# Eight matmuls with the high parts, then eight with the low parts, in place of eight pairs

## The chip, the cores and the metric

The kernel runs on one core of one Trainium2 chip. The metric is the device time of one execution in microseconds; lower is better. Three executions of the kernel before took 1486.58, 1487.91 and 1487.88 us, median 1487.88.

## The reference

One decoder block on 256 tokens of width 2048, in float32. What matters here is which matrix products it holds, and in which order:

```python
h = rmsnorm(x, attn_norm[i])
z = h @ w_in[i]                      # split into mq, mk, mv, mo, mi, mf, aq, ak, av, gm, ga
...                                  # mLSTM branch -> hm, attention branch -> ha
merged = (jax.nn.sigmoid(gm) * (hm @ w_up_m[i])
          + jax.nn.sigmoid(ga) * (ha @ w_up_a[i]))
x = x + merged @ w_out[i]
h = rmsnorm(x, mlp_norm[i])
x = x + jnp.square(jax.nn.relu(h @ w_ff1[i])) @ w_ff2[i]
h = rmsnorm(x, ple_norm[i])
x = x + jax.nn.sigmoid(h @ w_ple_gate[i]) * (p[i] @ w_ple_proj[i])
return rmsnorm(x, final_norm)
```

`w_ff1` is 2048 x 8192 and `w_ff2` 8192 x 2048; these two hold most of the arithmetic.

## The kernel before

**Split numbers.** A float32 value is held as two `float32r` values, high and low, whose sum is close to it. The product of a weight and an activation is taken as high x high + high x low + low x high. An activation tile `blk` is 128 x 512: columns 0 to 255 (`[:, 0:T]`, T = 256 tokens) hold the high part, columns 256 to 511 the low part. So one matmul with the weight's high part `h` as the stationary operand and the whole `blk` as the moving one (512 columns) gives high x high and high x low, side by side in one PSUM bank, and one with the weight's low part `l` and the left half of `blk` (256 columns) adds low x high to the left half.

**Chunks.** All weights are read in an order set by `plan()`, in chunks of 128 x 1024 (512 KB), two to a DMA. For chunk i+3 (`LOOK` = 3), `prep` lets ACT cast the chunk to `wh` (L182) and `prep_rest` lets DVE subtract to get `wl` (L190). There are four buffers each of `wh` and `wl`. The loop in `run()` goes through the chunks; for each it emits the PE's matmuls, then side work (`side()`), then the evacuation of banks that are complete.

**Two kinds of group.** In the groups named in `ROWS` (av, mv, mo, gm, um, ga, ua) the activations are stationary and the weights move, always 512 columns; the change doesn't touch them. In all other groups, called tile groups here (mq, mk, gate, aq, ak, wo, f1, f2, pp, pg), a chunk holds eight 128 x 128 weight tiles, called units: eight steps of the contraction into one PSUM bank (four outputs with two steps each for pp). Per unit the PE gets the high matmul and then the low one. Two groups differ: gate has no low matmul, and the last group, pg 3 (`narrow`), takes the high x high and high x low products as two matmuls of 256 columns, so that a unit is three matmuls of 256 columns. Every matmul has its own weight load (LDWEIGHTS, PEld in the profile).

**What sets the order.** Each engine runs its instructions in the order in which the loop emits them. Beside the loop, generators (attention, mLSTM, merge, statistics) put their work between chunks by a planner that keeps its own clock per engine; they put some matmuls and transposes on the PE, always between chunks. `wo` 0, the first group after the merge, takes its first four chunks in the order 0, 2, 1, 3 (`turn`), since its chunks 1 and 3 need the blocks that the merge makes last. `f2` needs the blocks `hid` that f1 makes, f1 the blocks `u2` that `next_operand` makes after wo.

Of the kernel before, what the change touches and what calls it, by code (L numbers as in the profile page):

```python
# [24 lines left out]
T = 256  # L25
# [26 lines left out]
def plan():  # L52

    g = []
    for n in range(2):
        g.append(("av", n))
    g += [("mq", 0), ("mk", 0), ("gate", 0), ("mv", 0), ("mv", 1), ("mo", 0), ("mo", 1)]
    for n in range(2):
        g += [("aq", n), ("ak", n)]
    for n in range(4):  # L60
        g += [("gm", n), ("um", n)]
    for n in range(4):
        g += [("ga", n), ("ua", n)]
    for n in range(4):
        g.append(("wo", n))
    for j in range(4):
        g += [("f1", 4 * j + n) for n in range(4)] + [("f2", 4 * j + n) for n in range(4)]
    for n in range(4):
        g += [("pp", n), ("pg", n)]
    return g  # L70


def turn(name, n, c):


    return (0, 2, 1, 3)[c] if (name, n) == ("wo", 0) and c < 4 else c
# [43 lines left out]
class Block:  # L120
# [788 lines left out]
    def run(self):  # L909
        nc, d = self.nc, self.d  # L910
        groups = plan()
        chunks = []
        for name, n in groups:
            c = {"gate": 2, "um": 4, "ua": 4, "pp": 1}.get(name, 8)
            chunks += [(name, n, i, c) for i in range(c)]
        self.nchunk = len(chunks)
        self.names = [c[0] for c in chunks]
        assert self.nchunk == 2 * d["w"].shape[0]
        self.stage, self.w, self.val, self.acc, self.rb, self.rcol = {}, {}, {}, {}, {}, {}
        self.summed = {}  # L920
        self.opd = {k: {} for k in ("u1", "u2", "u3", "hm", "ha", "mg", "p")}
        for j in range(4):
            self.opd["hid", j] = {}

        self.ones = self.cp.tile([128, 128], F32, name="ones")
        nc.vector.memset(self.ones, 1.0)
        self.warm_up()
        nc.scalar.preload_act_table_set("sqrt_and_others")
        self.x = {q: self.new4() for q in range(4)}
        self.dma(0, False)  # L930
        self.load_x(0, 0, 1)
        self.cols = self.cp.tile([128, NCOL], F32, name="cols")
        nc.scalar.dma_start(out=self.cols, in_=d["cols"])
        self.load_w(0, 0, 512)
        self.load_x(0, 1, 2)
        self.load_w(0, 512, 1024)
        self.load_x(0, 2, 3)
        self.load_w(0, 1024, 1536)
        self.load_x(0, 3, 4)
        self.load_w(0, 1536, 2048)  # L940
        for i in range(2, 8):
            if i < 2 * STAGE and i % 2 == 0:
                self.dma(i // 2, False)
            self.load_x(i // 2, 2 * (i % 2), 2 * (i % 2) + 2)
            if i < 2 * STAGE:
                self.load_w(i // 2, 1024 * (i % 2), 1024 * (i % 2) + 1024)
        self.con = self.cp.tile([128, NCON], F32, name="con")
        self.ident = self.con[:, K_ID:K_ID + 128]
        self.maskA = self.con[:, K_CA:K_CA + 256]
        self.maskB = self.con[:, K_CB:K_CB + 384]  # L950
        self.ones4 = self.cp.tile([4, T], F32, name="ones4")
        nc.vector.memset(self.ones4, 1.0)

        def load_u(k):
            self.opd["u1"][k] = self.blk()
            self.split(self.opd["u1"][k], self.xt(k), self.col(C_G1 + k))

        for i in range(LOOK):
            self.prep(i, 2)
            l, s, h = self.rest  # L960
            self.rest = None
            for k in range(2):
                load_u(2 * i + k)
                c = slice(512 * k, 512 * k + 512)
                self.copy(h[:, c], s[:, c])
                self.tt(l[:, c], s[:, c], h[:, c].bitcast(F32), OP.subtract)
            if i == 1:
                self.dma(STAGE)
        self.spawn(self.first_stats())
        self.spawn(self.tables())  # L970
        banks, acc = {}, {}
        for i, (name, n, c, nch) in enumerate(chunks):
            self.now = i
            if 2 * i + 7 < 16:
                load_u(2 * i + 6)
                load_u(2 * i + 7)
            if c == 0 and name == "ua":
                self.x[n] = self.new4()
                self.load_x(n, 0, 4)
            if i == 2:  # L980
                nc.sync.dma_start(out=self.con, in_=d["con"])
            if c == 0 and (name, n) == ("f2", 8):
                self.spawn(self.load_p())
            self.prep(i + LOOK)
            h, l = self.w.pop(i)
            src = self.opd[self.operand(name, n)]
            units, out = self.units(name, turn(name, n, c)), []
            for m, k in units:
                while k not in src:
                    self.force((name, n, c))  # L990
            if name in ROWS:
                nk = self.depth(name)
                if c == 0:
                    banks = [self.new_bank() for _ in range(2)]
                order = [(u, p, b) for u in range(2) for p in range(3) for b in range(2)]
                if c == nch - 1:
                    order = [(u, p, b) for b in range(2) for u in range(2) for p in range(3)]
                for u, p, b in order:
                    k = units[u][1]
                    wt = (h, h, l)[p][:, 512 * u:512 * u + 512]  # L1000
                    o = T * (p == 1) + 128 * b
                    self.mm(banks[b], src[k][:, o:o + 128], wt, start=k == 0 and p == 0,
                            stop=k == nk - 1 and p == 2)
                if c == nch - 1:
                    f = {"av": self.evac_v, "mv": self.evac_v, "mo": self.evac_o}
                    out.append((f.get(name, self.evac_t), name, n, banks))
            else:
                nk = self.depth(name)
                for u, (m, k) in enumerate(units):
                    if k == 0:  # L1010
                        acc[m] = self.new_bank()
                    ps = acc[m]
                    wc = slice(128 * u, 128 * u + 128)
                    a = src[k]
                    if self.narrow(name, n):
                        self.mm(ps[:, 0:T], h[:, wc], a[:, 0:T], start=k == 0, stop=False)
                        self.mm(ps[:, 0:T], h[:, wc], a[:, T:], start=False, stop=False)
                    else:
                        self.mm(ps, h[:, wc], a, start=k == 0,
                                stop=name == "gate" and k == nk - 1)  # L1020
                    if name != "gate":
                        self.mm(ps[:, 0:T], l[:, wc], a[:, 0:T], start=False, stop=k == nk - 1)
                    if k == nk - 1:
                        out.append((self.evac, name, n, m, ps))
            self.side()
            self.prep_rest(i + LOOK)
            for f, *args in out:
                f(*args)
        while self.tasks:
            self.force("end")  # L1030
        self.finish()
# [65 lines left out]
```

## Time and profile before

| | |
|---|---|
| three executions | 1486.58, 1487.91, 1487.88 us |
| the profiled execution | 1489.35 us, its span 1487.3 us |
| PE (matmuls) busy | 1472.3 us, 99% of the span |
| PEld (weight loads) busy | 1274.1 us, 86% |
| DVE, ACT busy | 992.0 us (67%), 736.4 us (50%) |
| granted TensorE clock | 0.996 of full speed in the mean |
| HBM | 187 GB/s over the span |

A matmul is recorded from its start to a modelled end, and the next one starts before that end. So the time that a matmul takes from the PE is read here as the distance between the starts of neighbours, not from its recorded duration.

### The profile page before, as it was taken

The page shows a single profiled execution, that of the slowest core. Times are in us where ns is not written, and L with a number is a line of the kernel's source. Part 1 is how long each engine was busy: PE and PEld are TensorE (multiplying, and loading weights), DVE is VectorE, ACT ScalarE, POOL GpSimd, SP SyncE. Part 2 cuts the span into 40 slices and gives each one's busy share as a digit, 9 for nine tenths or more (in the row PEclk, how much of TensorE's full clock was granted, in tenths as well). Part 3 has the DMA queues.
Part 4 walks back from the last instruction along what each step waited for, and adds up shares of the span by engine and source line. Part 5 has one row for each costly group of instructions (what it writes and reads, how often), then busy time and mean ns, then how long its engine had stood idle before and what let it go on. Part 6 is the DMA issues. An engine that isn't in the chain of part 4 may idle for free.

```text
span 1487.3 us, 19861 instructions
## 1 busy us (share of the span) xinstructions
PE 1472.3 (99%) x7996; PEld 1274.1 (86%) x7996; DVE 992.0 (67%) x1479; ACT 736.4 (50%) x1026; POOL 0.2 (0%) x4
## 2 busy tenths in 40 slices
PE   9999999999999999999999999999999999999996
PEld 7888888888888888888888888888888888888886
DVE  7686558875445556777766677656766667777785
ACT  7565654554444444455443454334444345555663
POOL 0000000000000000000000000000000000000000
PEclk9999999999999999999999999999999999999998
DMA  8554454444555554545455555555554555555551
GB/s 316 190 198 169 162 194 170 171 170 171 198 198 205 193 221 173 198 170 198 181 191 194 188 184 195 199 184 184 198 198 180 195 190 182 194 199 184 184 198 57
DMA packets 41467, 279.89 MB, mean 188 GB/s; under 512 B 4736, under 2 KB 5536, under 8 KB 8608
## 3 DMA queue, kind: packets, MB, share of 16 engines
q1 hardware_dynamic: 41232, 278.58, 52.3%
q8 instruction: 62, 1.02, 0.3%
q14 instruction: 29, 0.24, 0.1%
q10 hardware_dynamic: 144, 0.06, 0.0%
HBM read 276.52 MB, written 2.10 MB: 187 GB/s over the span
## 4 chain that ended last, share of the span: by engine, by line
PE 98%; DVE 1%; DMA 0%; ACT 0%; SPq 0%; issue 0%; DVEq 0%
PE acc L222 98%; PE acc L226 1%; DMA wst<-w 0%; DVE g L190 0%; ACT wh L182 0%; ACT blk L182 0%; DVE blk L190 0%; ACT L867 0%; SPq L360 0%; DVE rd L190 0%; DVE z L190 0%; ACT sq L178 0%; SPq L329 0%; ACT z L178 0%; DVEq L1092 0%
## 5 line engine op out<-in xcount | busy, mean ns | idle before, releaser
L222 PE MATMUL acc<-blk,wh 128*128 128x512 f32 (+1 forms) x3056 | 1041.7, 388 | 0.7 <-DVE blk L190 0.7
L222 PE MATMUL acc<-blk,wl 128*128 128x256 f32 x2976 | 832.4, 280 | 0.0
L190 DVE TENSOR_TENSOR wl<-wst,wh 128x1024 fp32r<-128x1024 f32 (+1 forms) x519 | 630.8, 1217 | 302.3 <-ACT wh L182 292.0
L182 ACT CAST wh<-wst 128x1024 fp32r<-128x1024 f32 (+1 forms) x521 | 544.6, 1046 | 461.5 <-PE acc L222 402.0
L222 PEld LDWEIGHTS acc<-blk,wh 128*128 128x128 f32 x3056 | 568.0, 187 | 124.3 <-DVE blk L190 1.4
L222 PEld LDWEIGHTS acc<-blk,wl 128*128 128x128 f32 x2976 | 562.0, 189 | 0.2
L222 PE MATMUL acc<-wh,blk 128*128 128x512 f32 x1152 | 318.7, 392 | 0.5 <-ACT wh L182 0.4
L222 PEld LDWEIGHTS acc<-wh,blk 128*128 128x128 f32 x1152 | 215.3, 188 | 45.5 <-ACT wh L182 1.6
L222 PE MATMUL acc<-wl,blk 128*128 128x512 f32 x576 | 184.8, 390 | 0.0
L222 PEld LDWEIGHTS acc<-wl,blk 128*128 128x128 f32 x576 | 108.0, 188 | 23.2 <-DVE wl L190 0.4
L182 ACT COPY lo<-acc 128x256 f32<-128x256 f32 (+1 forms) x118 | 43.0, 372 | 153.5 <-PE acc L222 153.5
L190 DVE TENSOR_TENSOR g<-g,acc 128x256 f32<-128x256 f32 (+2 forms) x166 | 72.1, 437 | 48.6 <-PE acc L222 45.9
L190 DVE TENSOR_TENSOR z<-acc,lo 128x256 f32<-128x256 f32 x76 | 32.3, 424 | 67.1 <-ACT lo L182 67.1
L182 ACT CAST blk<-z 128x256 fp32r<-128x256 f32 x64 | 26.0, 406 | 29.0 <-DVE z L201 29.0
L190 DVE TENSOR_TENSOR z<-z,rb 128x256 f32<-128x256 f32 x76 | 32.3, 425 | 3.2 <-ACT rb L182 0.6
L201 DVE SCALAR_TENSOR_TENSOR z<-z 128x256 f32<-128x256 f32 x64 | 27.3, 426 | 2.2
L178 ACT ACTIVATE sq<-g 128x256 f32<-128x256 f32 x64 | 25.9, 409 | 5.2 <-DVE g L190 4.5
L190 DVE TENSOR_TENSOR blk<-z,blk 128x256 fp32r<-128x256 f32 x64 | 26.7, 417 | 0.0
L190 DVE TENSOR_TENSOR nacc<-nacc,sq 128x256 f32<-128x256 f32 x59 | 24.8, 421 | 2.4 <-ACT sq L178 1.5
L178 ACT ACTIVATE blk<-g,cols 128x256 fp32r<-128x256 f32 x48 | 23.9, 508 | 3.0 <-DMA cols<-cols 1.5
L201 DVE SCALAR_TENSOR_TENSOR blk<-g,cols,blk 128x256 fp32r<-128x256 f32 x48 | 22.6, 479 | 3.6 <-ACT blk L178 3.6
L182 ACT CAST blk<-acc 128x256 fp32r<-128x256 f32 x24 | 9.0, 373 | 26.5 <-PE acc L226 13.1
(118 smaller groups left out, 333.6 us busy)
## 6 DMA issues: line engine op xcount, KB each, us to landing
wst<-w SPq DMA_DIRECT2D x256, 1024.0 KB, 4.8
wst<-w SPq DMA_DIRECT2D x4, 512.0 KB, 6.8
g<-x SPq DMA_DIRECT2D x4, 512.0 KB, 5.7
g<-x SPq DMA_DIRECT2D x6, 256.0 KB, 6.8
out_dram<-g SPq DMA_DIRECT2D x3, 512.0 KB, 2.8
wst<-w SPq DMA_DIRECT2D x4, 256.0 KB, 5.5
g<-x SPq DMA_DIRECT2D x4, 128.0 KB, 5.1
con<-con SPq DMA_DIRECT2D x1, 385.0 KB, 8.1
```

What stands on the lines that cost most here:

```text
L178: self.nc.scalar.activation(out, in_, func, **kw)
L182: self.nc.scalar.copy(out, in_)
L190: self.nc.vector.tensor_tensor(out, a, b, op=op)
L201: self.nc.vector.scalar_tensor_tensor(out, a, s, b, op0, op1)
L222: self.nc.tensor.matmul(out, lhsT=lhsT, rhs=rhs, start=start, stop=stop)
L226: self.nc.tensor.transpose(out, in_, ident)
```

## The change

In each chunk of a tile group the loop over the units now runs twice: first it emits all high matmuls (the 512-column ones, or the two of 256 columns in pg 3), then all low ones. The instructions, their number, operands and sizes stay as they are. Evacuation is still noted when the last step of a bank has its low matmul.

```diff
-                for u, (m, k) in enumerate(units):
-                    if k == 0:
-                        acc[m] = self.new_bank()
-                    ps = acc[m]
-                    wc = slice(128 * u, 128 * u + 128)
-                    a = src[k]
-                    if self.narrow(name, n):
-                        self.mm(ps[:, 0:T], h[:, wc], a[:, 0:T], start=k == 0, stop=False)
-                        self.mm(ps[:, 0:T], h[:, wc], a[:, T:], start=False, stop=False)
-                    else:
-                        self.mm(ps, h[:, wc], a, start=k == 0,
-                                stop=name == "gate" and k == nk - 1)
-                    if name != "gate":
-                        self.mm(ps[:, 0:T], l[:, wc], a[:, 0:T], start=False, stop=k == nk - 1)
-                    if k == nk - 1:
-                        out.append((self.evac, name, n, m, ps))
+                for low in (False, True):
+                    for u, (m, k) in enumerate(units):
+                        if k == 0 and not low:
+                            acc[m] = self.new_bank()
+                        ps = acc[m]
+                        wc = slice(128 * u, 128 * u + 128)
+                        a = src[k]
+                        if low:
+                            if name != "gate":
+                                self.mm(ps[:, 0:T], l[:, wc], a[:, 0:T], start=False,
+                                        stop=k == nk - 1)
+                            if k == nk - 1:
+                                out.append((self.evac, name, n, m, ps))
+                        elif self.narrow(name, n):
+                            self.mm(ps[:, 0:T], h[:, wc], a[:, 0:T], start=k == 0, stop=False)
+                            self.mm(ps[:, 0:T], h[:, wc], a[:, T:], start=False, stop=False)
+                        else:
+                            self.mm(ps, h[:, wc], a, start=k == 0,
+                                    stop=name == "gate" and k == nk - 1)
```

On the PE, the third chunk of `wo` 0 stood like this before, behind the merge's eight transposes (L226). `acc_4596` is the PSUM bank, `wh_4575` and `wl_4576` are the chunk's high and low weights, the `blk` tiles the merged blocks 8 to 15; block 12 is `blk_4644` and block 15, the last to be made, `blk_4661`:

```order
L226 MATMUL acc_4653<-con_119,g4_4516 128x128 x4
L222 MATMUL acc_4596<-blk_4397,wh_4575 128x512
L222 MATMUL acc_4596<-blk_4397,wl_4576 128x256
L222 MATMUL acc_4596<-blk_4400,wh_4575 128x512
L222 MATMUL acc_4596<-blk_4400,wl_4576 128x256
...
L222 MATMUL acc_4596<-blk_4658,wh_4575 128x512
L222 MATMUL acc_4596<-blk_4658,wl_4576 128x256
L222 MATMUL acc_4596<-blk_4661,wh_4575 128x512
L222 MATMUL acc_4596<-blk_4661,wl_4576 128x256
L222 MATMUL acc_4621<-blk_4397,wh_4593 128x512
```

And now, in the same place:

```order
L226 MATMUL acc_4653<-con_119,g4_4516 128x128 x4
L222 MATMUL acc_4596<-blk_4397,wh_4575 128x512
L222 MATMUL acc_4596<-blk_4400,wh_4575 128x512
...
L222 MATMUL acc_4596<-blk_4658,wh_4575 128x512
L222 MATMUL acc_4596<-blk_4661,wh_4575 128x512
L222 MATMUL acc_4596<-blk_4397,wl_4576 128x256
L222 MATMUL acc_4596<-blk_4400,wl_4576 128x256
...
L222 MATMUL acc_4596<-blk_4661,wl_4576 128x256
L222 MATMUL acc_4621<-blk_4397,wh_4593 128x512
```

The matmul that needs block 15 moved from the fifteenth place of the chunk to the eighth, and behind it stand eight low matmuls where one stood.

In the last chunk of pg 3, the end of the PE's work on weights, these rows stood before (a row with x2 is the high x high and the high x low product of one unit):

```order
L222 MATMUL acc_12781<-blk_11730,wh_12719 128x256 x2
L222 MATMUL acc_12781<-blk_11730,wl_12720 128x256
L222 MATMUL acc_12781<-blk_11784,wh_12719 128x256 x2
L222 MATMUL acc_12781<-blk_11784,wl_12720 128x256
L222 MATMUL acc_12846<-ones_78,nacc_11916 128x1
```

And now:

```order
L222 MATMUL acc_12781<-blk_11784,wh_12719 128x256 x2
L222 MATMUL acc_12781<-blk_11424,wl_12720 128x256
...
L222 MATMUL acc_12781<-blk_11730,wl_12720 128x256
L222 MATMUL acc_12781<-blk_11784,wl_12720 128x256
L222 MATMUL acc_12846<-ones_78,nacc_11916 128x1
```

All matmuls of this chunk have 256 columns in both; only their order moved, and the last one is the same.

## Rows read from the trace of the kernel before

**Rows 1.** The page: busy time by engine; the chain that ended last.

```profile
PE 1472.3 (99%) x7996; PEld 1274.1 (86%) x7996; DVE 992.0 (67%) x1479; ACT 736.4 (50%) x1026; POOL 0.2 (0%) x4
PE 98%; DVE 1%; DMA 0%; ACT 0%; SPq 0%; issue 0%; DVEq 0%
```

**Rows 2.** Waits of the PE and one of ACT: total us, times, longest.

```profile
PE acc L222 <- DVE blk L190: 0.7, 2, 0.5
...
ACT wh L182 <- PE acc L222: 402.0, 301, 2.7
```

**Rows 3.** Matmuls and weight loads by shape: count, busy us, mean recorded ns.

```profile
L222 PE MATMUL acc<-blk,wh 128*128 128x512 f32 x2928 | 1018.7, 393 | 0.7 <-DVE blk L190 0.7
L222 PE MATMUL acc<-blk,wl 128*128 128x256 f32 x2976 | 832.4, 280 | 0.0
...
L222 PEld LDWEIGHTS acc<-blk,wl 128*128 128x128 f32 x2976 | 562.0, 189 | 0.2
```

**Rows 4.** Timeline, PE, in f1: pairs (start, recorded us).

```profile
699.82 0.39 PE L222 MATMUL acc<-blk,wh 128*128 128x512 f32 x1
700.05 0.28 PE L222 MATMUL acc<-blk,wl 128*128 128x256 f32 x1
...
705.72 0.39 PE L222 MATMUL acc<-blk,wh 128*128 128x512 f32 x1
```

**Rows 5.** One stretch of f1 and f2: PE busy, matmuls, granted clock, DMA share.

```profile
700.00:900.00 200.00, 200.00 (x1155) 1.00 0.53 190
```

**Rows 6.** Timeline, PE, gate: sixteen 512-column matmuls behind pairs, from two windows.

```profile
96.50 3.82 PE L222 MATMUL acc<-blk,wh 128*128 128x512 f32 x16
...
98.11 2.20 PE L222 MATMUL acc<-blk,wh 128*128 128x512 f32 x9
100.15 0.39 PE L222 MATMUL acc<-wh,blk 128*128 128x512 f32 x1
```

**Rows 7.** Timeline, PE, start of pg 3: 256-column matmuls behind pairs.

```profile
1448.86 0.40 PE L222 MATMUL acc<-blk,wh 128*128 128x256 f32 x2
...
1449.80 0.28 PE L222 MATMUL acc<-blk,wl 128*128 128x256 f32 x1
1450.16 0.28 PE L222 MATMUL acc<-blk,wl 128*128 128x256 f32 x1
...
1451.96 0.28 PE L222 MATMUL acc<-blk,wl 128*128 128x256 f32 x1
```

**Rows 8.** Timeline, PE: first pair of wo, and the end of its sixteenth.

```profile
566.77 0.39 PE L222 MATMUL acc<-blk,wh 128*128 128x512 f32 x1
...
572.42 1.04 PE L226 MATMUL acc<-con,g 128*128 128x128 f32 x8
```

**Rows 9.** Timeline, PE, in aq/ak: eleven pairs.

```profile
198.13 0.39 PE L222 MATMUL acc<-blk,wh 128*128 128x512 f32 x1
...
202.00 0.40 PE L222 MATMUL acc<-blk,wh 128*128 128x512 f32 x1
```

**Rows 10.** Timeline, PE, third chunk of wo 0 [idle before, releaser].

```profile
573.21 0.47 PE L222 MATMUL acc<-blk,wh 128*128 128x512 f32 x1
...
576.88 0.50 PE L222 MATMUL acc<-blk,wh 128*128 128x512 f32 x1 [0.24 <-DVE blk L190]
577.22 0.28 PE L222 MATMUL acc<-blk,wl 128*128 128x256 f32 x1
577.34 0.40 PE L222 MATMUL acc<-blk,wh 128*128 128x512 f32 x1
```

**Rows 11.** Timeline, DVE: the merge's last block.

```profile
576.40 0.42 DVE L190 TENSOR_TENSOR blk<-acc,blk 128x256 fp32r<-128x256 f32 x1 [0.44 <-ACT blk L182]
```

**Rows 12.** Timeline, PE, f2's second chunk (751.82 starts it), and DVE's last hid block.

```profile
751.82 0.39 PE L222 MATMUL acc<-blk,wh 128*128 128x512 f32 x1
...
754.25 0.39 PE L222 MATMUL acc<-blk,wh 128*128 128x512 f32 x1
...
752.05 0.42 DVE L190 TENSOR_TENSOR blk<-z,blk 128x256 fp32r<-128x256 f32 x1
```

## Prediction

> **What bounds the kernel now.** I read the page first: the PE's matmuls are busy for 1472.3 of 1487.3 us and the chain of waits runs through the PE for 98% of the span [rows 1]. Then the waits: the PE waited for a block of an operand twice, 0.7 us in all [rows 2]. So in the stages that matter nothing is late; the PE goes from one matmul to the next, and the time is the number of matmuls times the distance between their starts. The table by shape gives the numbers: 2976 low matmuls, of which 64 are in pg 3 (eight chunks of eight units), so 2912 pairs of a 512-column and a 256-column matmul, or 364 chunks of eight pairs [rows 3]. The recorded durations there (393 and 280 ns) overlap and are no price. The price is in the timeline: in f1 seventeen pairs take 705.72 - 699.82 = 5.90 us, 347.1 ns a pair, the high matmul holding the PE for about 230 ns and the low one for about 117 [rows 4]; over 200 us 1155 matmuls ran, 173.2 ns each or 346.3 a pair [rows 5]. I take the middle, 346.7 ns. The granted clock there is 1.00, that is the level of 2.4 GHz, where 512 columns are 213.3 ns and 256 are 106.7, 320.0 together; so each matmul costs some 13.3 ns over its columns. The question is whether that surplus depends on the neighbour.
>
> **The change part by part.** No instruction is added or dropped. What is new is a high matmul behind a high one and a low one behind a low one, and the trace has both in other groups. The gate group has no low matmuls, so there sixteen high ones follow each other: the first seven take 98.11 - 96.50 = 1.61 us, 230 ns each, and the last nine 2.04 us, 226.7 each [rows 6]. In pg 3 all matmuls have 256 columns: the first eight take 0.94 us, 118 ns each, and later fifteen take 1.80 us, 120.0 each [rows 7]. So a run needs some eight matmuls to settle into its pace, and a chunk's runs are just that long.
>
> Settled, a chunk would take 8 x 226.7 + 8 x 120.0 = 2773.6 ns, and eight pairs take 8 x 346.7 = 2773.6: no difference at all. With the starts of the two runs instead, it is 1.61 + 0.23 = 1.84 us and 0.94 us, 2.78 us, so +6 ns a chunk. I take this one, since in the new order every run is a start behind the other kind, as those two were: 364 x 6 ns = +2.2 us. Its bounds mix the rows: high runs settled and low ones at their start give 960 - 940 = 20 ns less a chunk, -7.3 us; high runs at their start and low ones settled give 1840 - 1813.6 = 26 ns more, +9.5 us.
>
> Not all pairs run at 346.7 ns now. In wo sixteen pairs take 572.42 - 566.77 = 5.65 us, 353.1 each [rows 8], and in aq/ak eleven take 3.87 us, 351.8 each [rows 9]. Nothing waits there; the pairs have settled into a slower rhythm than in f1. If the new order has one pace everywhere, wo's 256 pairs win 256 x 6.4 ns = 1.6 us, and the 256 of aq/ak up to 256 x 5.1 ns = 1.3 us; I take half of the latter, since other matmuls come between there and the rhythm changes: together -2.3 us, with 0 (the slow rhythm comes back in the runs) and -2.9 us as bounds.
>
> One wait grows. In the third chunk of wo 0 the PE stands before block 15, which DVE finishes at 576.40 + 0.42 = 576.82 us [rows 11]; the high matmul starts at 576.88, its low one at 577.22, the next chunk at 577.34 [rows 10]. When block 15 is made depends on ACT and DVE, which do the same work in the same order there. In the new order the eighth high matmul waits for it, having come to it even earlier, and eight low matmuls follow, where one followed: 7 x 0.12 = +0.84 us, with little room to either side (0.8 to 0.9).
>
> Other hand-overs have cover. The last `hid` block is done at 752.05 + 0.42 = 752.47 us; the chunk that needs it starts at 751.82 and comes to it at 754.25 now, and would at 751.82 + 7 x 0.23 = 753.43, still 0.96 us behind it [rows 12]. What is queued behind such a wait would be the rest of the chunk and all later chunks. The cast of `wh` for chunk i+3 waits on the PE for 402 us in all [rows 2]: it needs the buffer of chunk i-1, whose last high matmul now ends seven low ones earlier, so the cast can start up to 0.9 us earlier. I cost this at nothing, since the PE didn't wait for casts in the stages at issue. The evacuation waits for the chunk's last low matmul as before. `wl` is needed later than before. The transposes and the end of the kernel stand at the same chunk boundaries. In pg 3 the order changes between matmuls of one size: 0. The weight DMAs hang on DVE's `wl`, which keeps its place: 0.
>
> Sum: +2.2 - 2.3 + 0.84 = +0.7 us. Against the profiled execution's own 1489.35 us that is 1490.1; this execution is 1.5 us above the median of the three timed ones, and the terms are differences, so I put them on the median: 1487.88 + 0.7 = **1488.6 us**, no change that a measurement of this kernel can tell (0.2%, 3 us).
>
> **A rule weighed.** Each matmul brings its own weight load, recorded at 189 ns [rows 3], longer than the 120 ns between two low matmuls [rows 7]. The Trainium skill (page "TensorE: Matmul & The Clock Gate", section "LDWEIGHTS (loading the stationary operand)") gives a load as its columns over 1.2 GHz, so an estimate of 107 ns for 128 columns, as long as the streaming of 256 columns. By that a run of low matmuls has no cover left for its loads, where in the pair every second load lies under a long matmul; but eight loads would take 0.86 us, less than the 0.94 to 0.96 that eight low matmuls take in the trace, so the sum would stay as it is. It makes a bound by loads (the last rival) less likely, not more.
>
> **Rivals.**
> - *The high runs never settle (slower).* Each high run starts behind a low one, pays the start of gate, and the low runs don't give it back because they settle quickly. For: after pairs the gate run needed seven matmuls to settle, a whole chunk's run. Against: the low run of pg 3 had a short start of its own. It decides from +12 ns a chunk (+4.5 us, +3.0 with the other terms); at +20 ns it is 364 x 20 ns = 7.3, so 7.3 - 2.3 + 0.84 = +5.8 us: 1493.7 us; at the bound of +26 ns, 1495.9.
> - *The low runs stay short (faster).* The low matmuls keep to the 118 ns or less of their start and the high ones settle at once: at -10 ns a chunk -3.6 - 2.3 + 0.84 = -5.1 us, 1482.8 us. For: 117 and 118 ns both occur [rows 4, 7]. Against: the pairs already have the 117 ns, paid for by 230 ns on the high one.
> - *Hand-overs become waits (slower).* At four starts of f2 and one of f1 the last block would be late by the time that it is needed earlier: up to 5 x 0.84 = 4.2 us on the sum, 1492.8 us. Against: 0.96 us are left at the one shown.
> - *Loads bound the low runs (slower).* If a load had to end before the next began, eight would take 8 x 189 ns = 1.51 us instead of 0.96: 364 x 0.55 = +200 us, 1689 us. Against: 120 ns in pg 3, with a load for each.
>
> **How the numbers follow.** My forecast (X, the change of a chunk, from -3 to +12 ns) has 0.56; unsettled high runs 0.28; short low runs 0.11; hand-overs 0.03; loads 0.02. Faster by over 0.2% is the second rival, 0.11; slower is the first, third and fourth, 0.33; the rest is no change. The range reaches from 1484.5 (about -5 ns a chunk) to 1494 (about +21 ns): it leaves out the far half of the second rival, the far end of the first, and the fourth.
>
> **What would show it.** In f1, eight highs followed by eight lows, with a chunk (first high to the next first high) of 2.77 to 2.79 us. Highs that go from about 230 ns down to 227, lows at 116 to 120. In wo chunks of the same length as in f1, not 2.82 us. In the third chunk of wo 0 the eighth high matmul waiting at 576.9 us less what was won before, and the next chunk 0.84 us later behind it than now. No new wait of the PE for a block at f2. I am wrong if a chunk in f1 takes over 2.79 or under 2.765 us, since 364 such chunks carry any error of the pace, or if the PE waits elsewhere.

## The result: slower by half a percent, against a forecast of no change

The changed kernel took 1495.0 us in the median of four executions (1494.37 to 1495.79), the kernel before 1487.6 in four beside it: ratio 1.0052, 95% interval 1.0037 to 1.0067. The forecast was 1488.6, with a range up to 1494.0 and a chance of 0.33 for slower. The profiled execution of the changed kernel took 1495.79 us with a span of 1493.7, so the two profiles are 6.4 us apart.

High and low matmuls are called highs and lows below. A run is a stretch of one kind; it has settled once the distance from start to start is steady, and the matmuls up to there are its start.

The page after, in the places of [rows 1]: PE's share is the same, and so is the number of matmuls; what was gained or lost was gained or lost in the distance between them.

```profile
PE 1478.5 (99%) x7996; PEld 1280.5 (86%) x7996; DVE 982.7 (66%) x1479; ACT 730.9 (49%) x1026; POOL 0.2 (0%) x4
```

Where the 6.4 us are is read from marks that both programs have: the merge's last transposes (L226), and the statistics' matmuls behind wo, f2 and pg, each the first row of its group. Before, on the PE:

```profile
572.42 1.04 PE L226 MATMUL acc<-con,g 128*128 128x128 f32 x8
...
664.97 0.50 PE L222 MATMUL acc<-ones,nacc 128*128 128x1 f32 x4
1375.82 0.50 PE L222 MATMUL acc<-ones,nacc 128*128 128x1 f32 x4
1471.88 0.50 PE L222 MATMUL acc<-ones,nacc 128*128 128x1 f32 x4
```

And after:

```profile
572.16 1.03 PE L226 MATMUL acc<-con,g 128*128 128x128 f32 x8
...
666.05 0.50 PE L222 MATMUL acc<-ones,nacc 128*128 128x1 f32 x4
1382.03 0.50 PE L222 MATMUL acc<-ones,nacc 128*128 128x1 f32 x4
1478.59 0.50 PE L222 MATMUL acc<-ones,nacc 128*128 128x1 f32 x4
```

Up to the first mark the two are even (-0.26 us here, +0.28 in a second profile of the changed kernel). From there to the end of wo it is 93.89 us for 92.55 (+1.34), through f1 and f2 715.98 for 710.85 (+5.13), through pp and pg 96.56 for 96.06 (+0.50); what follows is 0.32 us shorter. The 5.13 us are 256 chunks at **+20.0 ns** each.

That balance hides a gain that has nothing to do with pace. The four small transposes of the mLSTM's gates stand one chunk later in the changed kernel. Before:

```profile
124.73 0.48 PE L226 MATMUL acc<-con,g 4*128 4x4 f32 x4
...
126.29 1.57 PE L222 MATMUL acc<-g,g 128*128 128x256 f32 x8
```

After:

```profile
127.55 0.40 PE L226 MATMUL acc<-con,g 4*128 4x4 f32 x4
...
128.86 0.48 PE L222 MATMUL acc<-g,g 128*128 128x256 f32 x1
```

From the transposes to the matmuls behind them it is 1.31 us for 1.56. Between the gate group and aq 0 both profiles of the changed kernel are 0.26 us shorter than the kernel before, whose own profiles agree there within 0.02 us; the kernel with runs of 16 (below) has the transposes in their old place and gains nothing there. No run shows why they moved.

The PE's waits between 20 and 1470 us, after, are those ahead of the merge's last blocks and no other:

```profile
PE acc L222 <- DVE blk L190: 1.3, 3, 0.7
```

One chunk of f1 after, in the place of [rows 4]. The timeline joins equal neighbours into one row, so the same chunk is shown from three starting points, parted by dots; a row counts the matmuls from its start on (start, recorded us):

```profile
706.05 2.00 PE L222 MATMUL acc<-blk,wh 128*128 128x512 f32 x8
...
707.21 0.84 PE L222 MATMUL acc<-blk,wh 128*128 128x512 f32 x3
707.89 1.11 PE L222 MATMUL acc<-blk,wl 128*128 128x256 f32 x8
...
708.00 1.00 PE L222 MATMUL acc<-blk,wl 128*128 128x256 f32 x7
708.84 0.63 PE L222 MATMUL acc<-blk,wh 128*128 128x512 f32 x2
```

The first five highs take 707.21 - 706.05 = 1.16 us, 232 ns each; the last three 0.68, 226.7 each: the high run settles at its sixth matmul, three before it ends; in [rows 6] the gate group's had settled by its eighth. The first low takes 0.11 us, the other seven 0.84, 120 each. The low run has one short matmul, not eight, as at the start of pg 3 [rows 7].

In wo, the clock. The windows show PE busy, matmuls, granted clock and DMA share around the wait for the merge's last block, before:

```profile
574.00:577.30 3.30, 2.58 (x14) 1.00 0.02 5
577.30:580.60 3.30, 3.30 (x21) 1.00 0.51 129
```

After:

```profile
574.00:577.30 3.30, 2.03 (x8) 1.00 0.00 0
577.30:580.60 3.30, 3.30 (x13) 0.50 0.53 149
580.60:584.00 3.40, 3.40 (x20) 0.98 0.41 169
```

The PE waits in the same stretch, but has fewer matmuls to put between the waits (8 for 14, busy 2.03 us for 2.58), and then the granted clock is 0.50, the 1.2 GHz level, for some 3 us. In that time it does 13 matmuls, where it did 21.

### The profile page after: what moved, and what is told of

It is laid out like the page before. It is cut to its first block, busy times and chain, and to the rows that moved or that the text cites. A ratio compares the mean times of both kernels' runs of the same rounds, so it can differ in the third digit from the quotient of the medians.

```text
span 1493.7 us, 19862 instructions
## 1 busy us (share of the span) xinstructions
PE 1478.5 (99%) x7996; PEld 1280.5 (86%) x7996; DVE 982.7 (66%) x1479; ACT 730.9 (49%) x1026; POOL 0.2 (0%) x4
## 4 chain that ended last, share of the span: by engine, by line
PE 98%; DVE 0%; DMA 0%; ACT 0%; SPq 0%; issue 0%; DVEq 0%
PE acc L222 98%; PE acc L226 1%; DMA wst<-w 0%; DVE g L190 0%; ACT wh L182 0%; ACT blk L182 0%; DVE blk L190 0%; ACT L867 0%; SPq L360 0%; DVE rd L190 0%; DVE z L190 0%; ACT sq L178 0%; SPq L329 0%; ACT z L178 0%; DVEq L1096 0%
## 5 line engine op out<-in xcount | busy, mean ns | idle before, releaser
L222 PE MATMUL acc<-blk,wh 128*128 128x512 f32 (+1 forms) x3056 | 753.3, 389 | 1.3 <-DVE blk L190 1.3
L222 PEld LDWEIGHTS acc<-blk,wh 128*128 128x128 f32 x3056 | 543.9, 189 | 97.1 <-DVE blk L190 2.3
L222 PEld LDWEIGHTS acc<-blk,wl 128*128 128x128 f32 x2976 | 405.9, 191 | 28.4
L222 PE MATMUL acc<-blk,wl 128*128 128x256 f32 x2976 | 415.5, 283 | 0.0
```

Source lines behind the costliest of these rows:

```text
L222: self.nc.tensor.matmul(out, lhsT=lhsT, rhs=rhs, start=start, stop=stop)
```

## The experiments

All are the kernel with another order of the matmuls within a chunk; `low, u` in the diffs is one step (low part or not, unit u). A ratio is to the kernel before on the same chip, whose median was 1487.6 to 1489.2 there. The f1/f2 column is the time between the two marks around these stages in the profile, and its distance from the 710.85 us of before, by chunk. The kernel before has times that differ by 0.1% from execution to execution (the last experiment), so the ratios carry that mixture; the f1/f2 column doesn't. The runs of 16, 4 and 2, and those begun in mid-chunk, keep wo 0 in pairs as well, so that the clock's fall stays out of them. The expectations for runs of 16 and in mid-chunk build on the 1492.7 us that were expected for wo 0 in pairs, which took 1493.89.

| kernel | median us | ratio (95%) | f1/f2 us | ns a chunk |
|---|---|---|---|---|
| before, pairs | 1487.6 | | 710.85 | |
| changed, runs of 8 | 1495.0 | 1.0052 (1.0037 to 1.0067) | 715.98 | +20.0 |
| wo 0 in pairs, else runs of 8 | 1493.89 | 1.0038 (1.0026 to 1.0051) | 715.98 | +20.0 |
| runs of 16 | 1490.54 | 1.0014 (1.0005 to 1.0022) | 713.44 | +10.1 |
| runs of 8, begun in mid-chunk | 1494.1 | 1.0040 (1.0026 to 1.0054) | 715.97 | +20.0 |
| runs of 4 | 1498.37 | 1.0068 (1.0053 to 1.0083) | 719.33 | +33.1 |
| runs of 2 | 1491.65 | 1.0022 (1.0013 to 1.0032) | 714.26 | +13.3 |
| changed, again | 1494.95 | 1.0046 (1.0032 to 1.0059) | 715.98 | +20.0 |

**wo 0 back in pairs.** Does the wait for the merge's last block cost more than the low matmuls behind it?

```diff
+        if (name, n) == ("wo", 0):
+            return pairs
+        return runs
```

> The changed kernel, but wo 0 stays in pairs. Theory: the wait for block 15 of the merge cost more than its 0.84 us, because the clock fell to half behind it (granted 0.50 from 577.3 to 580.6 us in the changed kernel's trace, some 1.6 us lost). Then both go: 1495.0 - 0.84 - 1.6 + 0.2 (wo 0 back in the slow rhythm of its pairs) = 1492.7 us, granted clock 1.00 in that stretch, next chunk of wo 0 at about 577.3 us less the shift at its start. Rival: the clock falls there for another reason, and only the 0.84 us go: 1494.3 us, clock 0.50 again.

The time is 1.1 us lower in the medians, which were taken at different times, and 2.2 lower in the profiled spans (1493.7 and 1491.5), where 2.2 were expected; the clock stayed at 1.00:

```profile
574.00:577.30 3.30, 2.57 (x14) 1.00 0.02 5
577.30:580.60 3.30, 3.30 (x20) 1.00 0.43 124
```

The profile bears the theory out; the median says less, 1493.89 for 1492.7 us. The granted clocks say why: of the four executions behind the median of 1495.0 us only the profiled one has a granted clock of 0.995 over its span, the other three have 0.996, so the median held little of the 1.6 us.

**The changed kernel again.** No edit.

> The changed kernel, unchanged, once more. Theory: every chunk of f1 and f2 again at 20 ns over eight fast pairs, whatever the execution; the clock's fall behind wo 0's wait may or may not come again, since its wait is near what the kernel before had without a fall: 1.6 us between the two. Against the kernel before on the same chip 1.004 to 1.006.

Its windows, in the same stretch:

```profile
574.00:577.30 3.30, 2.04 (x7) 1.00 0.00 0
577.30:580.60 3.30, 3.30 (x20) 1.00 0.30 87
```

The wait is the same (busy 2.04 of 3.30 us), the clock stayed at 1.00, and wo took 92.35 us for the 93.89 with the fall: 1.54 us for the fall. So it comes in some executions of the changed kernel; in the four profiles of the kernel before it was not seen. The executions without a trace say the same by their granted clock over the span: three of the nine of the changed kernel have 0.995 (1495.79, 1496.95, 1495.9 us, mean 1496.2), six have 0.996 or 0.997 (mean 1494.7), 1.6 us apart; none of the 59 of the kernel before that were timed beside the experiments is under 0.996, and none of the 34 with wo 0 in pairs and other groups in runs.

The wait itself, in this profile:

```profile
577.16 0.50 PE L222 MATMUL acc<-blk,wh 128*128 128x512 f32 x1 [0.36 <-DVE blk L190]
577.50 1.12 PE L222 MATMUL acc<-blk,wl 128*128 128x256 f32 x8
578.46 2.00 PE L222 MATMUL acc<-blk,wh 128*128 128x512 f32 x8
```

From the matmul that needs block 15 to the next chunk it is 1.30 us, where it was 577.34 - 576.88 = 0.46 us [rows 10]: +0.84 us. Without the clock's fall wo is 0.20 us shorter than in the profile before. That fits two terms: +0.84 us behind the wait, and -1.0 us from some 30 chunks at 2793 instead of 8 x 353.3 = 2827 ns.

**Runs of sixteen.** Is it the start of a run that costs, the chunk's boundary, or a high matmul behind a high one as such? The second chunk of each bank takes its lows first:

```diff
+        second = units[0][1] == 8
+        return [(not low, u) for low, u in runs] if second else runs
```

> As e1, but the second chunk of each bank takes its eight low matmuls first and then its highs, so that runs are sixteen long, with a chunk boundary in the middle of each low run and of every other high one (wo 0 in pairs). Theory: what costs is the start of a high run behind lows (+27 ns over the first five) and what a low run's start gives back is 7 ns; half the starts, so about 176 x 20 ns = 3.5 us less than e1: 1489.2 us. In the trace no slower matmuls at a chunk boundary inside a run. Rival boundary (the first matmuls of a chunk are slow because of new weight buffers or waits): as e1, 1492.7 us, slower matmuls at every chunk's start. Rival neighbour (a high matmul behind a high one costs more, wherever it stands): as e1 or slower.

Half the starts, half the cost: +10.1 ns a chunk for +20.0, and 3.35 us less in the medians than with wo 0 in pairs and runs of eight (3.5 expected). One period of f1:

```profile
707.54 3.82 PE L222 MATMUL acc<-blk,wh 128*128 128x512 f32 x16
711.20 2.08 PE L222 MATMUL acc<-blk,wl 128*128 128x256 f32 x16
713.11 0.40 PE L222 MATMUL acc<-blk,wh 128*128 128x512 f32 x1
```

Sixteen highs take 3.66 us, 0.03 over settled (3.63), and sixteen lows 1.91, 0.01 under settled (1.92). That is the same start once, in runs of twice the length. "Neighbour" and "boundary" both fall: there are more highs behind highs, and boundaries within runs.

**Runs of eight, begun in mid-chunk.** All tile groups but wo 0 and pp:

```diff
+        return ([(False, u) for u in range(4)] + [(True, u) for u in range(8)]
+                + [(False, u) for u in range(4, 8)])
```

> As e1, but each chunk is four highs, eight lows, four highs: runs of eight as in the changed kernel, with the starts in the middle of the chunks. Theory: same time as e1, 1492.7 us, with 233, 236, 228, 233, 231 ns on the fifth to eighth high of a chunk and on the first of the next one. Rival boundary: the slow matmuls stay at the chunk's first highs, and the time may go either way.

+20.0 ns a chunk, and the time of the run with wo 0 in pairs (1494.1 and 1493.89). In f1, where the chunk's boundary now stands in the middle of a run of highs:

```profile
706.08 2.00 PE L222 MATMUL acc<-blk,wh 128*128 128x512 f32 x8
707.92 1.12 PE L222 MATMUL acc<-blk,wl 128*128 128x256 f32 x8
708.87 0.63 PE L222 MATMUL acc<-blk,wh 128*128 128x512 f32 x2
```

Eight highs take 1.84 us and eight lows 0.95, as in the changed kernel. By place in the run the highs take 233, 236, 228, 232 and 231 ns in the mean of f1 and f2, then 227: the slow matmuls went along with the run's start.

**Runs of four and of two.**

The order with runs of four; for runs of two both 4s are a 2:

```diff
+        return [(low, u) for r in range(0, 8, 4) for low in (False, True)
+                for u in range(r, r + 4)]
```

> As e1, but four highs, four lows, four highs, four lows in each chunk. Theory (cost per start of a high run): two starts a chunk, each at least the first four of the changed kernel's highs (233 + 236 + 228 + 233 = 930 ns, 23 over the settled 907) less 7 for the lows, so +32 to +46 ns a chunk over pairs: 356 x that = 11.4 to 16.4 us on some 1486.6 (the pairs' time without the slow rhythm of wo and aq/ak): 1498 to 1503 us. Rival neighbour (cost per high behind a high, six of eight instead of seven): 1492 us. Rival boundary: as e1, 1492.7 us.

> As e1, but two highs, two lows and so on. Four starts a chunk: if each costs what its first two matmuls cost in the changed kernel (233 + 236 = 469 ns, 16 over settled) less 7 for the low's start, +36 ns a chunk, 1499 us; if a run this short falls into a rhythm of its own as pairs do, anything from 1486 (the pairs' fast rhythm) to 1499. Rival neighbour (four highs of eight behind a high): 4/7 of 7.3 us, 1490.8 us.

Four: 1498.37 us, at the low edge of what was expected (+33.1 ns, expected +32 to +46). In f1 of that kernel:

```profile
706.25 1.09 PE L222 MATMUL acc<-blk,wh 128*128 128x512 f32 x4
707.18 0.64 PE L222 MATMUL acc<-blk,wl 128*128 128x256 f32 x4
707.66 1.09 PE L222 MATMUL acc<-blk,wh 128*128 128x512 f32 x4
708.59 0.63 PE L222 MATMUL acc<-blk,wl 128*128 128x256 f32 x4
709.06 1.09 PE L222 MATMUL acc<-blk,wh 128*128 128x512 f32 x4
```

The four highs take 0.93 us where settled ones take 0.907; they never settle. The lows take 0.48 and 0.47. With runs of two the price falls again, to +13.3 ns, and 1491.65 us: four starts a chunk don't cost four times a start. So "a price per start" held for eight and sixteen and nearly for four; below it a run has a rhythm of its own, as pairs have. Here my number (1499 us) was an end of a wide range, and the time lay within it. The rival "neighbour" was nearer with 1490.8 us, but for runs of four it asked for 1492 us and falls by that.

**The pairs' slow rhythm.** Pairs run at 346.7 ns in f1 and ran at 353.1 in wo [rows 4, 8]. Can the order of a few chunks set it?

```diff
+        first = (name, n, nth) in (("mq", 0, 0), ("aq", 0, 0), ("wo", 0, 0), ("wo", 0, 3))
+        return runs if first else pairs
```

> The kernel before (pairs), with the eight-and-eight order in four chunks alone: the first of mq 0, of aq 0 and of wo 0, and the fourth of wo 0. Theory: the rhythm of the pairs (346.7 or 353.3 ns) is set by how they are entered; entered behind a settled run of lows they take the fast one. Then the 28 later chunks of wo win 53 ns each, 1.5 us, the four chunks some 10 ns each against slow pairs, aq/ak up to 0.3: 1487.6 - 1.9 = 1485.7 us, wo pairs at 346.7 ns. Rival: wo's operands set the rhythm (353.3 ns again), 1487.6 us.

This theory failed: 1489.61 us, ratio 1.0008 (0.9999 to 1.0017). Behind the run in wo 0 the pairs are slow:

```profile
581.13 0.39 PE L222 MATMUL acc<-blk,wh 128*128 128x512 f32 x1
...
589.61 0.40 PE L222 MATMUL acc<-blk,wh 128*128 128x512 f32 x1
```

24 pairs in 8.48 us, 353.3 each. The next kernel disturbs the order at one place in each of wo 1, 2 and 3. There `half(2)` is two highs, two lows, twice, and `half(4)` four highs, four lows; both go on in pairs:

```diff
+        if (name, n, nth) == ("wo", 1, 1):
+            return [(not low, u) for low, u in pairs]
+        if (name, n, nth) == ("wo", 2, 0):
+            return half(2)
+        if (name, n, nth) == ("wo", 3, 0):
+            return half(4)
```

> The kernel before (pairs), with one disturbed chunk in each of wo 1, 2 and 3: in wo 1 the second chunk takes each unit's low matmul before its high one; in wo 2 the first chunk begins with two highs, two lows, twice; in wo 3 with four highs, four lows. Theory: the pairs' rhythm (346.7 or 353.3 ns) is a matter of how they are entered, not of wo's operands; at least one of the three disturbances throws the slow rhythm over to the fast one (or back), and it then stays for the rest of the group. Rival: the operands set it, and the pace after each disturbance is that of before it.

The pace went from 346.7 to 353.3 ns at the first place, back to 346.7 at the second and to 353.3 at the third (1488.16 us in its one execution). The first place begins with a low behind a low (row of 593.56) and ends with a high behind a high (row of 596.23):

```profile
593.56 0.40 PE L222 MATMUL acc<-blk,wl 128*128 128x256 f32 x2
593.80 0.40 PE L222 MATMUL acc<-blk,wh 128*128 128x512 f32 x1
...
595.88 0.40 PE L222 MATMUL acc<-blk,wh 128*128 128x512 f32 x1
...
596.23 0.62 PE L222 MATMUL acc<-blk,wh 128*128 128x512 f32 x2
...
596.80 0.40 PE L222 MATMUL acc<-blk,wh 128*128 128x512 f32 x1
...
597.86 0.40 PE L222 MATMUL acc<-blk,wh 128*128 128x512 f32 x1
```

Inside the disturbed chunk six pairs take 2.08 us (347 each), behind it three take 1.06 us (353). So the pace changed at its end, where two highs stand in a row, and not at its start, where two lows do; and the operands don't set the rhythm. Then the order that had thrown it to fast was put at the head of wo 1, 2 and 3:

```diff
+        if name == "wo" and n > 0 and nth == 0:
+            return [(low, u) for q in (0, 2) for low in (False, True)
+                    for u in (q, q + 1)] + pairs[8:]
```

> The kernel before (pairs), but the first chunk of wo 1, 2 and 3 begins with two highs, two lows, two highs, two lows. In the last look this threw wo's pairs from 353.3 to 346.7 ns. Theory: it does so whenever they come in the slow rhythm, and leaves the fast one alone; then wo 1 to 3 run at 346.7 ns in every execution, 1.3 us less than in the slow executions of the kernel before, and the times no longer fall in two groups: about 1487.5 to 1488 us where the kernel before has 1487.4 and 1489.3, ratio 0.9992. Rival: it throws the rhythm over each time, fast to slow too: wo 1 and 3 in one rhythm and wo 2 in the other, no gain in the median.

Neither came: wo was fast up to the first such chunk and slow behind all three (352.4 to 353.9 ns in means of eight pairs), 1488.9 us, ratio 1.0005 (0.9996 to 1.0014). What decides at the entry is open. No version here beats the kernel before.

**The kernel before, again.** Its own times lie mostly near 1487.4 or near 1489.3 us. No edit; three single executions, each with a profile.

> The kernel before, unchanged, once more. Its times fell in two groups on the last chip, about 1487.4 and 1489.3 us. Theory: the two are the two rhythms of wo's pairs (and those of aq/ak); wo's 256 pairs at 353.3 instead of 346.7 ns are 1.7 us. Then a profile with a time near 1487.4 shows wo at 346.7 ns a pair, one near 1489.3 shows 353.3. Rival: the 2 us lie elsewhere (the start, the DMA), and wo's pace is the same in both.

> The kernel before, unchanged, to meet an execution of its faster group. Theory: at a time near 1487.4 us wo runs at 346.7 ns a pair, near 1489.3 at 353.3. Rival: wo's pace is the same at both times.

> The same once more, with the same expectation: near 1487.4 us wo at 346.7 ns a pair, near 1489.3 at 353.3; rival, the same pace at both.

At 1489.38 and 1489.29 us wo ran at 353.3 ns, at 1487.89 at 346.7. Two marks of the last, as above:

```profile
572.82 0.71 PE L226 MATMUL acc<-con,g 128*128 128x128 f32 x5
...
663.72 0.50 PE L222 MATMUL acc<-ones,nacc 128*128 128x1 f32 x4
```

90.90 us for 92.55 in the profile that the prediction was read from: 1.65 us, which is 256 pairs at 6.4 ns. The two groups are the two rhythms of wo, at least for the most part, as far as three profiles of the slower group and one of the faster can tell; the start and the end of the kernel differ by up to 0.6 us each among the four. So the profile read for the prediction was of the slower group, and the medians with which the result is compared mix both.

## Why the prediction was wrong

- *What bounds the kernel*: right. The PE's chain from matmul to matmul decided; between 20 and 1470 us the PE waited for nothing but the merge's last blocks (1.3 us), so no other hand-over became a wait (rival 3), and loads didn't bound the low runs (rival 4): seven lows at 120 ns. One premise was wrong, that the transposes stay at their chunk boundaries. Those of the mLSTM's gates came one chunk later, worth -0.26 us.
- *+6 ns a chunk*: this is the step that failed. It was put as "the starts of the two runs", 1.84 us for eight highs and 0.94 for eight lows. The highs were right: 707.89 - 706.05 = 1.84 us, 27 ns over settled. The lows took 0.95 us (708.84 - 707.89), 7 ns under settled, where 20 had been put. Half of that error is the state of the predecessor: pg 3's low run began behind pairs and ran short for eight matmuls, while in the new order a low run begins behind a *settled* high run, and only its first matmul is clearly short. The other half is rounding: the trace has 946 ns for pg 3's first eight, 14 under settled, and the difference of two rows with two decimals made 0.94 us of it. With 946 the forecast for a chunk would have been +12 ns and the time 1490.9 us, still under what was measured; 6 ns are little in one chunk and 2.2 us in 364. The measured sum is +20 ns, and 364 x 20 = 7.3 us for the 2.2 forecast. That is the point at which the first rival was priced (1493.7 us, 0.28), and its words hold: "the low runs don't give it back because they settle quickly"; only, the high runs do settle, at their sixth matmul, and start anew in every chunk.
- *-2.3 us from the slow rhythm*: right in size against the profile it was read from (behind the merge's wait the changed kernel's chunks of wo are at 2793 ns without the clock's fall; the 32 chunks of aq and ak are 0.02 us shorter in sum, where +20 ns each would be +0.64, so 0.66 came from their slow rhythm for the 0.65 that was put; another execution of the kernel before, with wo in the fast rhythm, was 1.65 us shorter there, where 1.6 was the term), but not to be had in the median, since the kernel before has the fast rhythm in wo anyway in part of its executions. The sum was put on 1487.88 us, a time of the faster group, where the 1.6 us of wo were most likely already had (those executions left no trace). This is a second slip, smaller than the first: 1487.88 + 7.3 - 0.65 + 0.84 = 1495.4 us, and 1495.0 was measured.
- *+0.84 us behind the merge's last block*: right in mechanism and, from the execution without the clock's fall, in size. What was missed is what can follow when the PE has less to do between its waits: a stretch at the 1.2 GHz level in some executions, 1.54 us. With wo 0 in pairs it did not come.
- *Sum*: with the measured price of a chunk the terms give 7.3 - 2.3 + 0.84 = +5.8 us, and +7.4 with the clock's fall. The profiles show +5.2 without (spans 1492.5 and 1487.3) and +6.4 with it (1493.7). Of the 0.6 and 1.0 us between, 0.26 are the transposes. Another 0.1 and 0.5 are at the start and the end, where the kernel before differs from itself by up to 0.6 us each. What is left, some 0.3 us in both, no run took apart.

## What to carry to other kernels

When the PE is the bound and nothing is late, the distance between matmuls is the price, and it depends on what ran before: read it in the order that will stand there, its predecessor's state included, not from the nearest stretch of the same shape. A run of one kind pays for its start, so count the starts: sixteen in a row cost half of eight, and strict alternation cost nothing here in its fast rhythm. A price that is multiplied by hundreds needs a long stretch, since rows with two decimals are off by up to 10 ns in a difference. Before a kernel is compared to a fraction of a percent, look whether its own times fall in groups, and which group the profile is from.

## What the runs showed of the hardware that was not expected

- A stream of matmuls with a weight load each falls into fixed rhythms, all at the granted clock 1.00: 512 columns at 226.7 ns, 256 at 120.0, pairs of both at 346.7 or at 353.3, and each stays until the order is broken, by another kind of matmul or by two highs in a row; a break doesn't always change it. The same pairs with the same operands held one rhythm in one execution and the other in the next (wo: 90.90 and 92.55 us).
- Entering a high run from lows costs 27 ns over the first five matmuls, whatever the chunk's boundary; the low run behind it gives 7 back, nearly all on its first. Why a start costs this, no run shows.
- By length of run the price of eight pairs' work is 0, +13, +33, +20, +10 ns for 1, 2, 4, 8, 16: it is highest at four, where the highs end before they have settled.
- The clock fell to the 1.2 GHz level behind a stretch in which the PE was busy 2.03 of 3.30 us, in one execution; in another with 2.04 of 3.30 it did not. By the granted clock over the span it fell in three of nine.
